# Two transformer layers with an S5 branch: a later-written input for the residual's scaling, the next layer's S5 operators and the gelu

## The chip, the cores and the metric

The kernel runs on one core of a Trainium2 chip, in one launch. The metric is the device time of that launch in microseconds (us); three runs of the kernel before are shown. Engines are called as in the profile: PE is the matrix engine (PEld its weight loads), DVE the vector engine, ACT the scalar engine, POOL is GpSimd, and SP issues most of the DMAs.

## The reference

Two layers run over 640 tokens, 128 context tokens and 512 latent ones, with 1024 channels. Each layer computes

- `h = x * (1 + scale1) + shift1`, and one product with `w_in`, whose columns are the input of the S5 branch, q, k and v of a windowed attention, q, k and v of a global attention, and three gates
- branch 0, a two-way S5 scan with small complex states, then `y = gelu(y)` and `y = y * sigmoid(y @ w_glu)`
- branch 1, the windowed attention (at most 128 tokens away, with the context's keys from a cache), and branch 2, the global attention; both have 8 heads of 64
- `merged = sum_k sigmoid(gate_k) * (branch_k @ w_br_k)` and `f = merged @ w_out`
- `x = LayerNorm(alpha * x + gate1 * f)`, then `x = LayerNorm(alpha * x + gate2 * relu(h2 @ w_up)^2 @ w_down)` with `h2 = x * (1 + scale2) + shift2`; the MLP has 4096 hidden columns

All of it is held in float32. The states and the keys and values of the context are outputs too.

## The kernel before, in words

**Tiles.** The tokens are `NT` = 5 tiles of 128: tile 0 is the context, 1 to 4 are the latent tokens. The layers are l = 0 and l = 1.

**Products.** A float32 operand is split in two rounded parts: `split` (L120) writes hi = copy(src) on ACT (L126) and lo = src - hi on DVE (L127); with `half` it also halves (L123, L124). Each product is three matmuls (hi with hi, hi with lo, lo with hi): L162 to L164 in `mm_fm`, L173 to L175 in `mm_tm`, L1247 to L1249 in the MLP's second product. `wtile` (L129) loads a raw weight tile and splits it into two `whi` and two `wlo` tiles, of which there are `WBUFS` = 4 each. A product's result goes to a p_g bank of PSUM (in the MLP to p_sc banks too).

**The order of work.** No order of the whole is written out by hand. A framework takes the program, gives each tile a buffer of its tag (`bufs` of them, handed out in the program's order), and puts every engine's instructions in one fixed order by a planned timeline, in which what comes earlier in the program has priority and what comes later fills in where nothing earlier can run. On the chip each engine's queue then runs strictly in that order, and an instruction waits for its inputs and its buffer.

**Around the gelu (`phase_a`).** In the program's order: the S5 scan, whose output is read back into `yT` (L1068); the windowed attention; the global attention (L1156), which writes `yg`; the gates of branch 1 (some were computed earlier and kept in DRAM, `AHEAD`), and branch 1's product (L1165); the gelu over `yT` in place (L1166); `split_y` into `ya` (L1168); four tiles of branch 0's gates, computed ahead and stored in DRAM (L1169); the GLU, two weight tiles and four channel tiles, each a product, a tanh on ACT into an `sg` tile of tag t640 (L1180, two such buffers) and an update of `yT` on DVE (L1182); `split_y` again (L1184); the fifth gate ahead (L1185); branch 0 (L1187), which fetches the stored gates into t640 buffers (L1111); the first gates of branch 2 into `gg`, a large tile in the buffer that `yT` had (L1188 to L1193); branch 2 (L1206), whose input is `yg`.

The attention (`attend`) works token tile by token tile, and in a tile by four pairs of heads. A pair's scores fill two p_sc banks, or three where there are five key blocks (there are three banks); row maxima on DVE (L950), their combination (L953 windowed, L958 global), the exponentials on ACT (L962, L964), transposes of P on PE (L971) into p_pt, a split of them, and the product with V. When a tile's four pairs are done, it is divided by the sums (L1001): for the global attention that is the last write of `yg[:, t]`.

**Around the MLP (`phase_b`).** After the product with `w_out` and the norm (L276 writes `x`), h2 is split into hh and hl. The MLP goes over e = 0 to 7: up(e), then down(e - 1), which from e = 1 on adds into `acc` (L1460; down(0) writes it). At e = 3 the program has the block that scales the residual, `x = x * (alpha g) + (alpha b)` in halves of 512 columns: ten multiplications (L1474) and ten additions (L1475) on DVE, with the two rows loaded by DMA and scaled by alpha on ACT (`rows`, L1220, for layer 0; `halves_of`, L1439, in four DMAs, for layer 1, where the MLP's products use a scheme with fewer multiplications). At e = 7 a like block of 20 operations, L1484 and L1485, prepares `acc` for the second norm. Layer 1's S5 operators are computed in layer 0's MLP: `both` (L1298) is a generator that `ahead()` advances one step per weight tile from down(0) on; it begins in `s5_prep` (L279) with three POOL copies (L288) and four DMAs of small inputs.

A POOL copy of one column into a tile that a DMA or another instruction then writes makes that instruction wait for what the copy reads.

Of the kernel before, what the change touches and what calls it, by code (L numbers as in the profile page):

```python
# [4 lines left out]
F32 = mybir.dt.float32  # L5
# [10 lines left out]
NT = 5  # L16
D = 1024
NCH = 84
ALPHA = (2.0 * DEPTH) ** 0.25
# [12 lines left out]
def net(tc, I, O, depth=DEPTH, dbg=None):  # L32
    nc = tc.nc
    V, S, G, T, SY = nc.vector, nc.scalar, nc.gpsimd, nc.tensor, nc.sync
    dbg = dbg or {}

    def ap(t, off, dims):
        return bass.AP(tensor=t.tensor, offset=t.offset + off, ap=[list(d) for d in dims])

    def bc(t, off, n):  # L40
        return ap(t, off, [[0, 128], [1, n]])

    def dump(name, t):
        if name in dbg:
            SY.dma_start(dbg[name], t)
# [11 lines left out]
    def pg():  # L57
        turn[0] += 1
        if mlp[0] == 2:
            return (psc, ppt, lambda: bank("g", 2), psc, ppv, ppt, lambda: bank("g", 2), psc)[turn[0] % 8]()  # L60
        return psc() if mlp[0] and turn[0] % 5 in (1, 3, 4) else bank("g", 2)
# [4 lines left out]
    def ppt():  # L66
        return bank("pt", 2)
# [61 lines left out]
    def wtile(src, K, slot=None):  # L129

        raw = raw_tile(src)
        out = []
        for i in range(2):
            if slot is not None:
                hi, lo = slot(), slot()
            else:
                hi = wp.tile([128, 512], F32R, name="whi", tag="whi", bufs=WBUFS)
                lo = wp.tile([128, 512], F32R, name="wlo", tag="wlo", bufs=WBUFS)
            cnt["w"] += 1
            split(hi, lo, raw[:, i * 512:(i + 1) * 512])  # L140
            hv, lv = (z.rearrange("p (k c) -> p k c", k=K // 2) for z in (hi, lo))
            out += [(hv[:, k], lv[:, k]) for k in range(K // 2)]
        return out

    def cols(ws, a, b):
        return [(x_[:, a:b], y_[:, a:b]) for x_, y_ in ws]
# [132 lines left out]
    def s5_prep(l, pp, pl_, keep, after=None, use=None):  # L279
# [5 lines left out]
        lre, lim, lst = t32("lre"), t32("lim"), t32("lst")  # L285
        if after is not None:
            for z in (lre, lim, lst):
                G.tensor_copy(z[:, 0:1], after)  # L288
        SY.dma_start(lre, I["lam_re"][:, l])
        SY.dma_start(lim, I["lam_im"][:, l])  # L290
        for d in range(2):
# [51 lines left out]
        k, r, a2, w = tmp  # L343
# [94 lines left out]
        for b in range(8):  # L438
# [4 lines left out]
            for r_ in range(2):  # L443
# [3 lines left out]
                p = pq()  # L447
# [66 lines left out]
    def phase_a(l, h):  # L514
# [8 lines left out]
        def f10(name):  # L523
            return qp.tile([128, 4 * 8 * NCH], F32, name=name, tag="F10", bufs=2)

        if l == 0:
# [39 lines left out]
            for g_ in range(4):  # L566
                if g_ < 3:
                    mods0(g_ + 1)
                for k in range(2 * g_, 2 * g_ + 2):
                    hf = xin.tile([128, NT, 128], F32, name="hf", tag="hf", bufs=2)  # L570
                    for t0, t1 in ((2, 5), (0, 2)):
                        p = ppt()
# [58 lines left out]
        for ft in range(4):  # L631
# [5 lines left out]
            for i, (t0, t1) in enumerate(SPLITS):  # L637
                n = (t1 - t0) * 128
                p = uacc[ft][i] if ws is None else pg()
# [178 lines left out]
        def gate(i, ft, out_fn, side=iter(())):  # L818

            ws = wtile(I["w_gate"][l, i * 8 + ft], 8)  # L820
            for t0, t1 in SPLITS:
                p = pg()
                n = (t1 - t0) * 128
                mm_fm(p[:, :n], ws, H, t0, t1)
                next(side, None)
                S.activation(out_fn(t0, t1), p[:, :n].rearrange("p (t n) -> p t n", n=128), AF.Tanh, scale=0.5)
# [212 lines left out]
        for b in range(8):  # L1039
# [8 lines left out]
            p = pg()  # L1048
# [18 lines left out]
        yT = f10("yT").rearrange("p (f t c) -> p f t c", f=4, t=8)  # L1067
# [12 lines left out]
        def t640(name):  # L1080
            return bp.tile([128, NT, 128], F32, name=name, tag="t640", bufs=2)
# [21 lines left out]
        def branch(i, acts, last=None, side=iter(()), ready={}):  # L1103
            for i2 in range(4):
                ws = wtile(I["w_br"][l, i, i2], 4)
                for f in range(2):
                    ft = 2 * i2 + f
                    pre = i == 1 or ft in ready
                    sg = mtv[:, ft] if i == 1 else ready[ft] if pre else t640("sg")
                    if i == 0 and ft < sum(AHEAD[l][4:]):  # L1110
                        SY.dma_start(sg.rearrange("p t n -> p (t n)"), s_d[l][0, ft])  # L1111
                    elif not pre:
                        gate(i, ft, lambda t0, t1: sg[:, t0:t1])
                    for t0, t1 in SPLITS:
                        p = pg()
                        n = (t1 - t0) * 128
                        mm_fm(p[:, :n], cols(ws, f * 128, f * 128 + 128), acts, t0, t1)
                        next(side, None)
                        V.scalar_tensor_tensor(sg[:, t0:t1], sg[:, t0:t1], 1.0, p[:, :n].rearrange("p (t n) -> p t n", n=128), op0=ALU.add, op1=ALU.mult)  # L1119
                    if i != 1:  # L1120
                        V.tensor_tensor(mtv[:, ft], sg, mtv[:, ft], op=ALU.add)
                    if last is not None:
                        last(ft)
# [31 lines left out]
        yg = f10("yg")[:, 0:2560].rearrange("p (t f n) -> p t f n", t=NT, f=4)  # L1155
# [7 lines left out]
        for ft in range(n1, 8):  # L1163
            gate(1, ft, lambda t0, t1: mtv[:, ft, t0:t1])
        branch(1, aw, side=mods)  # L1165
        S.activation(yT, yT, AF.Gelu_apprx_tanh)  # L1166
        dump("yT", yT)
        ya = split_y(False)  # L1168
# [2 lines left out]
        for i2 in range(2):  # L1171
            ws = wtile(I["w_glu"][l, i2], 4)
            for f in range(2):
                ft = 2 * i2 + f
                sg = t640("sg")
                for t0, t1 in SPLITS:
                    p = pg()
# [38 lines left out]
    def phase_b(l, M):  # L1216
        mp = tc.alloc_tile_pool(name=f"mp{l}", bufs=1, reuse_waits="tile")
        mlp[0] = True

        def rows(*srcs, scale=None):  # L1220

            r = mp.tile([128, 2, D], F32, name="rows", tag="rows", bufs=1)
            for i, (src, off) in enumerate(srcs):
                SY.dma_start(r[:, i], bc(src, off, D))
            if scale is not None:
                S.activation(r, r, AF.Copy, scale=scale)
            return r[:, 0], r[:, 1]
# [26 lines left out]
        x = mp.tile([128, NT, D], F32, name="x")  # L1254
        acc = mp.tile([128, NT, D], F32, name="acc")
# [26 lines left out]
        for t in range(NT):  # L1282
            p = pg()
# [14 lines left out]
        def both(l, pool, after):  # L1298
            kept = {}
            yield from s5_prep(l, pool, pool, kept, after)  # L1300
            yield from s5_tables(l, pool, kept)

        nxt = []
        if l + 1 < depth:
            nxt = [mods_steps(l + 1, range(3), lambda: mp.tile([128, 512], F32, name="mtmp", tag="mtmp", bufs=1),
                              lambda: mp.tile([128, 4, 128], F32, name="hf", tag="hf", bufs=2).rearrange("p a b -> p (a b)")), both(l + 1, mp, x[:, NT - 1, D - 1:D])]
        calls = [0]

        def ahead():
# [126 lines left out]
            def __getitem__(self, i):  # L1436
                return self.parts[i[1].start // 512]

        def halves_of(srcs, scale=None):  # L1439
            r = [Halves([mp.tile([128, 512], F32, name=n, tag=n, bufs=2) for _ in range(2)]) for n in ("gp", "rl")]  # L1440
            for z, (src, off) in zip(r, srcs):
                for i, y in enumerate(z.parts):
                    SY.dma_start(y, bc(src, off + 512 * i, 512))
                    if scale is not None:
                        S.activation(y, y, AF.Copy, scale=scale)
            return r
# [17 lines left out]
        ff = up(0)  # L1464
        for e in range(1, 8):
            if e == 3:

                if bil:
                    rg_, rb_ = halves_of(((I["ln1_g"], l * D), (I["ln1_b"], l * D)), scale=ALPHA)
                else:  # L1470
                    rg_, rb_ = rows((I["ln1_g"], l * D), (I["ln1_b"], l * D), scale=ALPHA)
                for t in range(NT):
                    for cs in (slice(0, 512), slice(512, 1024)):
                        V.tensor_tensor(x[:, t, cs], x[:, t, cs], rg_[:, cs], op=ALU.mult)  # L1474
                        V.tensor_tensor(x[:, t, cs], x[:, t, cs], rb_[:, cs], op=ALU.add)  # L1475
            if e == 7:

                if bil:
                    g2 = halves_of([(g_d[l], (2 + c) * D) for c in range(2)])
                else:  # L1480
                    g2 = rows(*((g_d[l], (2 + c) * D) for c in range(2)))
                for cs in (slice(0, 512), slice(512, 1024)):
                    for t in range(NT):
                        V.tensor_tensor(acc[:, t, cs], acc[:, t, cs], g2[0 if t == 0 else 1][:, cs], op=ALU.mult)  # L1484
                        V.tensor_tensor(acc[:, t, cs], acc[:, t, cs], x[:, t, cs], op=ALU.add)  # L1485
            nf = up(e)
            if e == 7 and bil:

                down(6, ff, (0,))
                f6 = ff  # L1490
            else:
                down(e - 1, ff)
            ff = nf
# [25 lines left out]
        if l + 1 == depth:  # L1519
            rg_, rb_ = ([mp.tile([128, 512], F32, name="lrow", tag="lrow", bufs=4) for _ in range(2)] for _ in range(2))  # L1520
# [3 lines left out]
        for t in range(NT):  # L1524
            for c in range(2):
                p = pg()
# [10 lines left out]
            else:  # L1537
                ve = ln_stat(st[t])
                o = O["xp"] if t == 0 else O["xs"][(t - 1) * 128:t * 128, :]
                for cs in (slice(0, 512), slice(512, 1024)):  # L1540
                    z = acc[:, t, cs]
# [15 lines left out]
    for l in range(depth):  # L1557
        M = phase_a(l, h)
        h = phase_b(l, M)
# [98 lines left out]
```

## Time and profile before

| | us |
|---|---|
| three runs | 2341.27, 2339.97, 2344.25 |
| median | 2341.27 |
| the profiled execution: its own time | 2345.22 |
| its span, first to last instruction | 2343.4 |
| PE busy | 2254.6 (96%) |
| DVE busy | 1568.1 (67%) |
| ACT busy | 1082.9 (46%) |
| POOL busy | 44.7 (2%) |
| mean granted clock of PE | 0.981 |

The profile is one execution. Busy time is the time in which an engine worked on at least one instruction; starts are counted from the span's beginning. The granted clock is a share of PE's full speed.

### The profile page before, as it was taken

What the parts mean: (1) busy time and instruction counts of PE and PEld (TensorE: products, weight loads), DVE (VectorE), ACT (ScalarE), POOL (GpSimd) and SP (SyncE); (2) the same over time, 40 slices, a digit from 0 to 9 for tenths busy, and PEclk for the clock granted to TensorE, in tenths of its full rate; (3) what the DMA queues carried; (4) which work ended last, traced back from release to release, by engine and by line L of the source; (5) the groups of instructions that cost most, each with busy time, mean ns of one, the idle gap of its engine ahead of it and who ended that gap; (6) DMA issues with size and microseconds to landing.
All of it is one profiled execution on the core that took longest, in us unless ns stands there. A gap on an engine that the chain in (4) does not pass through costs nothing.

```text
span 2343.4 us, 38521 instructions
## 1 busy us (share of the span) xinstructions
PE 2254.6 (96%) x14736; PEld 2040.4 (87%) x14736; DVE 1568.1 (67%) x3471; ACT 1082.9 (46%) x2572; POOL 44.7 (2%) x75
## 2 busy tenths in 40 slices
PE   7998999999998999999999999989999989999998
PEld 4997896899997988888888998989999879999986
DVE  6789954676358955455657598466763587776688
ACT  3455654674344443223224457456652356454441
POOL 0000100000000000000000001000000000000000
PEclk8998999999999999999999999999999999999999
DMA  7423366523242345344354522552212413222231
GB/s 268 119 81 106 108 179 229 198 72 98 73 154 65 94 172 175 127 156 160 135 176 142 162 63 88 158 182 77 86 53 80 171 37 99 77 77 83 83 106 62
DMA packets 124825, 283.16 MB, mean 121 GB/s; under 512 B 37057, under 2 KB 56641, under 8 KB 124641
## 3 DMA queue, kind: packets, MB, share of 16 engines
q1 hardware_dynamic: 124640, 280.70, 37.3%
q8 instruction: 116, 1.90, 0.3%
q14 instruction: 69, 0.56, 0.1%
HBM read 243.59 MB, written 41.25 MB: 122 GB/s over the span
## 4 chain that ended last, share of the span: by engine, by line
PE 82%; DVE 9%; DMA 5%; ACT 2%; issue 1%; SPq 1%; POOL 0%; DVEq 0%; ACTq 0%; POOLq 0%
PE p_g L162 8%; PE p_g L164 8%; PE p_g L163 8%; PE p_sc L1247 3%; PE p_sc L1249 3%; PE p_sc L1248 3%; PE p_sc L162 3%; PE p_sc L163 3%; PE p_sc L164 3%; PE p_pt L971 2%; PE p_g L1247 2%; PE p_g L1249 2%; PE p_g L1248 2%; PE p_g L173 2%; PE p_g L174 2%; PE p_g L175 2%
## 5 line engine op out<-in xcount | busy, mean ns | idle before, releaser
L126 ACT ACTIVATE whi<-raw 128x512 fp32r<-128x512 f32 x454 | 282.8, 631 | 408.7 <-PE p_g L1249 98.0
L127 DVE TENSOR_TENSOR wlo<-raw,whi 128x512 fp32r<-128x512 f32 x454 | 310.0, 688 | 229.7 <-ACT whi L126 220.6
L162 PE MATMUL p_g<-hh,whi 128*128 128x384 f32 (+1 forms) x1040 | 327.3, 315 | 2.3 <-ACT whi L126 1.2
L163 PE MATMUL p_g<-hl,whi 128*128 128x384 f32 (+1 forms) x1040 | 325.0, 313 | 2.8 <-DVE hl L127 2.8
L164 PE MATMUL p_g<-hh,wlo 128*128 128x384 f32 (+1 forms) x1040 | 324.4, 313 | 1.4 <-DVE wlo L127 1.2
L162 PEld LDWEIGHTS p_g<-hh,whi 128*128 128x128 f32 x1040 | 198.7, 191 | 8.0 <-ACT rl L1421 4.2
L163 PEld LDWEIGHTS p_g<-hl,whi 128*128 128x128 f32 x1040 | 198.9, 191 | 3.3 <-DVE hl L127 3.3
L164 PEld LDWEIGHTS p_g<-hh,wlo 128*128 128x128 f32 x1040 | 198.3, 191 | 2.5 <-DVE wlo L127 2.5
L162 PE MATMUL p_g<-act,whi 128*128 128x384 f32 x448 | 141.0, 315 | 5.6 <-DVE mt L1119 3.9
L127 DVE TENSOR_TENSOR pl<-p_pt,ph 128x512 fp32r<-128x512 f32 (+1 forms) x176 | 103.0, 589 | 58.1 <-ACT ph L126 44.7
L173 PE MATMUL p_g<-whi,hh 128*128 128x256 f32 x480 | 138.6, 291 | 1.1 <-DVE rt L742 0.7
L163 PE MATMUL p_g<-act,whi 128*128 128x384 f32 x448 | 139.5, 311 | 0.0
L164 PE MATMUL p_g<-act,wlo 128*128 128x384 f32 x448 | 138.7, 310 | 0.0
L174 PE MATMUL p_g<-wlo,hh 128*128 128x256 f32 x480 | 137.1, 288 | 1.1 <-DVE wlo L127 1.1
L175 PE MATMUL p_g<-whi,hl 128*128 128x256 f32 x480 | 136.7, 287 | 0.0
L163 PE MATMUL p_sc<-hl,whi 128*128 128x384 f32 (+1 forms) x384 | 121.5, 317 | 5.5 <-DVE hl L127 2.9
L126 ACT ACTIVATE ph<-p_pt 128x512 fp32r<-128x512 f32 (+1 forms) x176 | 90.7, 522 | 73.4 <-PE p_pt L971 71.3
L162 PE MATMUL p_sc<-hh,whi 128*128 128x384 f32 (+1 forms) x384 | 121.8, 319 | 0.4 <-ACT hh L126 0.4
L164 PE MATMUL p_sc<-hh,wlo 128*128 128x256 f32 (+1 forms) x384 | 120.7, 316 | 0.0
L950 DVE TENSOR_REDUCE part<-p_sc 128x1 f32<-128x384 f32 (+2 forms) x160 | 83.3, 526 | 34.2 <-PE p_sc L940 20.5
L971 PE MATMUL p_pt<-ident,P 128*128 128x128 f32 x576 | 96.6, 278 | 8.3 <-ACT P L962 6.3
L1247 PE MATMUL p_sc<-whi,ff 128*128 128x512 f32 x248 | 98.6, 400 | 0.0
(542 smaller groups left out, 5961.2 us busy)
## 6 DMA issues: line engine op xcount, KB each, us to landing
raw<-in_w_mod_dram SPq DMA_DIRECT2D x96, 512.0 KB, 3.9
raw<-in_w_up_dram SPq DMA_DIRECT2D x64, 512.0 KB, 3.7
raw<-in_w_down_dram SPq DMA_DIRECT2D x64, 512.0 KB, 3.6
raw<-in_w_gate_dram SPq DMA_DIRECT2D x48, 512.0 KB, 3.6
raw<-in_w_br_dram SPq DMA_DIRECT2D x24, 512.0 KB, 6.7
raw<-in_w_q_dram SPq DMA_DIRECT2D x16, 512.0 KB, 3.7
ctab_d<-ct SPq DMA_DIRECT2D x16, 512.0 KB, 2.6
tab<-ctab_d SPq DMA_DIRECT2D x16, 512.0 KB
```

The costliest lines, as they stand in the source:

```text
L126: S.activation(hi, src, AF.Copy)
L127: V.tensor_tensor(lo, src, hi, op=ALU.subtract)
L162: T.matmul(out, wh, tok(ah, t0, t1), start=(first and k == 0), stop=False)
L163: T.matmul(out, wh, tok(al, t0, t1), start=False, stop=False)
L164: T.matmul(out, wl, tok(ah, t0, t1), start=False, stop=(last and k == n - 1))
L173: T.matmul(out, ah, wh, start=(first and k == 0), stop=False)
L174: T.matmul(out, ah, wl, start=False, stop=False)
L175: T.matmul(out, al, wh, start=False, stop=(last and k == n - 1))
L971: T.transpose(p[:, (2 * (z - z0) + z_) * 128:(2 * (z - z0) + z_ + 1) * 128], Ps[z_][:, z * 128:(z + 1) * 128], ident)
L1247: T.matmul(banks[t], a_, wh, start=(k == 0), stop=False)
L1248: T.matmul(banks[t], a_, wl, start=False, stop=False)
L1249: T.matmul(banks[t], b_, wh, start=False, stop=(k == n - 1))
```

## The change

Four instructions or blocks are each given an input that is written later, by a small GpSimd copy into one of their operands.

- The three copies in `s5_prep` read one column of the last lo tile that up(0) writes, in place of the last column of the norm's output. The source is now a function, called when the generator starts, and `ff`, the output of up(0), is empty until then.
- A copy of one column of `yg`, token tile 4, into `yT` stands ahead of the gelu.
- The rows that scale the residual at e = 3 (layer 0) are first written by a copy that reads the last column of `acc`, token tiles 3 and 4.
- The four half rows of layer 1 are first written by copies that read the last column of `acc`, token tile 4.

```diff
@@ s5_prep
         if after is not None:
             for z in (lre, lim, lst):
-                G.tensor_copy(z[:, 0:1], after)
+                G.tensor_copy(z[:, 0:1], after())
         SY.dma_start(lre, I["lam_re"][:, l])
@@ phase_a
         branch(1, aw, side=mods)
+        G.tensor_copy(yT[:, 0, 0, 0:1], yg[:, NT - 1, 0, 0:1])
         S.activation(yT, yT, AF.Gelu_apprx_tanh)
@@ phase_b
-        def rows(*srcs, scale=None):
+        def rows(*srcs, scale=None, after=None):
             r = mp.tile([128, 2, D], F32, name="rows", tag="rows", bufs=1)
+            if after is not None:
+                G.tensor_copy(r[:, :, 0:1], after)
@@
+        ff = []
         if l + 1 < depth:
...
-both(l + 1, mp, x[:, NT - 1, D - 1:D])]
+both(l + 1, mp, lambda: ff[-1][1][:, NT - 1, 127:128].bitcast(F32))]
@@
-        def halves_of(srcs, scale=None):
+        def halves_of(srcs, scale=None, after=None):
...
+                    if after is not None:
+                        G.tensor_copy(y[:, 0:1], after)
                     SY.dma_start(y, bc(src, off + 512 * i, 512))
@@ e == 3
-                    rg_, rb_ = halves_of(..., scale=ALPHA)
+                    rg_, rb_ = halves_of(..., scale=ALPHA, after=acc[:, NT - 1, D - 1:D])
-                    rg_, rb_ = rows(..., scale=ALPHA)
+                    rg_, rb_ = rows(..., scale=ALPHA, after=acc[:, NT - 2:NT, D - 1:D])
```

## Rows read from the trace of the kernel before

**Rows 1.** The page's head and its first part.

```profile
span 2343.4 us, 38521 instructions
PE 2254.6 (96%) x14736; PEld 2040.4 (87%) x14736; DVE 1568.1 (67%) x3471; ACT 1082.9 (46%) x2572; POOL 44.7 (2%) x75
```

**Rows 2.** L1166, the gelu: duration ns min/median/max, first and last start us, forms.

```profile
L1166 ACT ACT_TABLE_LOAD  x2: 1283/1283/1283, 378.5 to 1535.4; - x2
L1166 ACT ACTIVATE yT<-yT x2: 2447/2450/2452, 379.8 to 1536.7; 128x2688 f32<-128x2688 f32 x2
```

**Rows 3.** L1001 in 340 to 700 us (layer 0) and 1490 to 1890 (layer 1).

```profile
L1001 DVE TENSOR_TENSOR yg<-yg,p_pt x5: 680/686/689, 403.1 to 574.6; 128x512 f32<-128x512 f32 x5
...
L1001 DVE TENSOR_TENSOR yg<-yg,p_pt x5: 677/687/690, 1569.8 to 1746.8; 128x512 f32<-128x512 f32 x5
```

**Rows 4.** L1180 of both layers, and L1111 of layer 0, in the same stretches.

```profile
L1180 ACT ACTIVATE sg<-p_g x8: 367/444/519, 496.6 to 518.8; 128x384 f32<-128x384 f32 x4, 128x256 f32<-128x256 f32 x4
...
L1180 ACT ACTIVATE sg<-p_g x8: 380/446/495, 1650.6 to 1671.5; 128x384 f32<-128x384 f32 x4, 128x256 f32<-128x256 f32 x4
...
L1111 SPq DMA_DIRECT2D sg<-s_d x5: 319/326/350, 512.1 to 547.1; - x5
```

**Rows 5.** L958, once per head pair, in 492 to 575 and in 1647 to 1750.

```profile
L958 DVE TENSOR_TENSOR stat<-part,ssq x7: 139/152/161, 497.8 to 556.4; 128x2 f32<-128x2 f32 x7
...
L958 DVE TENSOR_TENSOR stat<-part,ssq x8: 147/153/178, 1650.4 to 1728.6; 128x2 f32<-128x2 f32 x8
```

**Rows 6.** Windows, all instructions: us, PE, PEld, DVE, ACT, POOL busy, PEclk, DMA share, GB/s.

```profile
492.00:575.00 83.00, 82.49 (x599) 80.52 (x598) 65.60 (x135) 53.73 (x131) 0.00 (x0) 1.00 0.28 86
1647.00:1747.00 100.00, 98.56 (x712) 97.52 (x712) 70.84 (x143) 60.23 (x149) 0.00 (x0) 1.00 0.22 69
```

**Rows 7.** The same windows, instructions that touch p_g alone (no POOL column).

```profile
492.00:575.00 83.00, 61.12 (x371) 54.09 (x370) 6.54 (x14) 5.66 (x13) 1.00 0.28 86
1647.00:1747.00 100.00, 73.56 (x446) 66.77 (x447) 6.73 (x14) 6.95 (x16) 1.00 0.22 69
```

**Rows 8.** L953, once per pair of the windowed attention, in 1452 to 1480.

```profile
L953 DVE TENSOR_TENSOR stat<-part,nsink x5: 152/161/161, 1454.6 to 1477.3; 128x2 f32<-128x2 f32 x5
```

**Rows 9.** L288, the first of the three POOL copies.

```profile
L288 POOL COPY lre<-x x1: 671/671/671, 748.3 to 748.3; 128x1 f32<-128x1 f32 x1
```

**Rows 10.** Tile yT in 340 to 700: ACT's half of the split behind the gelu.

```profile
L126 ACT ACTIVATE act<-yT x8: 416/764/1146, 442.9 to 453.9; 128x128 fp32r<-128x128 f32 x4, 128x512 fp32r<-128x512 f32 x4
```

**Rows 11.** PE's waits in 1515:1560, 733:765, 1890:1920: us in total, times, longest.

```profile
PE p_pt L971 <- ACT P L962: 2.5, 1, 2.5
...
PE p_sc L163 <- DVE hl L127: 2.9, 1, 2.9
PE p_g L163 <- DVE hl L127: 1.8, 1, 1.8
...
PE p_sc L163 <- DVE mv L267: 2.6, 1, 2.6
```

**Rows 12.** Windows as in rows 6: norm to MLP, windowed attention, MLP.

```profile
745.00:765.00 20.00, 14.97 (x74) 13.65 (x73) 19.79 (x43) 8.76 (x19) 1.87 (x3) 0.83 0.11 24
1890.00:1912.00 22.00, 15.73 (x72) 13.32 (x71) 17.94 (x45) 13.60 (x28) 1.46 (x2) 0.77 0.09 25
1454.00:1478.00 24.00, 23.22 (x152) 21.45 (x153) 12.42 (x29) 13.84 (x36) 0.00 (x0) 0.86 0.42 131
800.00:830.00 30.00, 30.00 (x168) 24.47 (x167) 24.70 (x55) 12.33 (x25) 0.00 (x0) 1.00 0.44 144
2043.00:2068.00 25.00, 25.00 (x171) 24.91 (x170) 21.30 (x39) 17.57 (x36) 0.00 (x0) 1.00 0.30 89
2254.00:2279.00 25.00, 24.72 (x169) 24.46 (x168) 24.34 (x46) 14.88 (x31) 0.00 (x0) 1.00 0.38 127
```

**Rows 13.** L1474 in 730 to 770, and L1485 in 2200 to 2290.

```profile
L1474 DVE TENSOR_TENSOR x<-x,rows x10: 684/686/691, 745.2 to 759.2; 128x512 f32<-128x512 f32 x10
...
L1485 DVE TENSOR_TENSOR acc<-acc,x x10: 683/685/687, 2241.5 to 2264.8; 128x512 f32<-128x512 f32 x10
```

More of the change, by code (lines that the diff above doesn't have):

```diff
@@ L1303, in phase_b @@
         nxt = []
+        ff = []
         if l + 1 < depth:
             nxt = [mods_steps(l + 1, range(3), lambda: mp.tile([128, 512], F32, name="mtmp", tag="mtmp", bufs=1),
-                              lambda: mp.tile([128, 4, 128], F32, name="hf", tag="hf", bufs=2).rearrange("p a b -> p (a b)")), both(l + 1, mp, x[:, NT - 1, D - 1:D])]
+                              lambda: mp.tile([128, 4, 128], F32, name="hf", tag="hf", bufs=2).rearrange("p a b -> p (a b)")), both(l + 1, mp, lambda: ff[-1][1][:, NT - 1, 127:128].bitcast(F32))]
         calls = [0]
@@ L1468, in phase_b @@
                 if bil:
-                    rg_, rb_ = halves_of(((I["ln1_g"], l * D), (I["ln1_b"], l * D)), scale=ALPHA)
+                    rg_, rb_ = halves_of(((I["ln1_g"], l * D), (I["ln1_b"], l * D)), scale=ALPHA, after=acc[:, NT - 1, D - 1:D])
                 else:
-                    rg_, rb_ = rows((I["ln1_g"], l * D), (I["ln1_b"], l * D), scale=ALPHA)
+                    rg_, rb_ = rows((I["ln1_g"], l * D), (I["ln1_b"], l * D), scale=ALPHA, after=acc[:, NT - 2:NT, D - 1:D])
                 for t in range(NT):
```

## The prediction, made before the change was timed

> **What bounds the kernel now.** I read the page's sums first [rows 1]: PE is busy 2254.6 of the span's 2343.4 us, DVE 67%, ACT 46%, POOL 2%. So PE is idle for only 88.8 us in all, an edit can win no more than that, and it can lose wherever it takes from PE the matmuls that cover someone's wait. So for each edit I asked what PE does meanwhile.
>
> The instructions of the gelu's line come next [rows 2]: a table load at 378.5 and 1535.4 us, and a gelu of 2.45 us right behind it, at 379.8 and 1536.7. The scaling of the attention output, once per token tile, shows where the global attention stands [rows 3]: its last write starts at 574.6 in layer 0 and at 1746.8 in layer 1. **Today the gelu runs about 200 us before the attention ends**, in both layers. In between lies what hangs on it: the GLU's tanhs run from 496.6 and from 1650.6 [rows 4], and the first gate that was computed ahead is fetched behind them at 512.1, for branch 0. The attention's head pairs go on through all that: 7 of them from 497.8 to 556.4, and 8 from 1650.4 to 1728.6 [rows 5]. In these stretches PE is busy 82.49 of 83 us and 98.56 of 100 [rows 6], but of that 61.12 and 73.56 us are p_g products (GLU, branch and gates), not attention [rows 7]. The attention's own share is 82.49 - 61.12 = 21.4 us and 98.56 - 73.56 = 25.0 us. Covered so, a pair comes every (556.4 - 497.8) / 6 = 9.8 us; its PE work is only 21.4 / 7 = 3.1 us.
>
> **The gelu's edit, part 1: the attention loses its cover.** The copy reads token tile 4 of yg, so the gelu waits for the attention's last write. Queued behind the gelu, by data or by buffers, are split_y, the GLU (its two weight tiles fill all four weight slots, so the later gate's weights can't come first), the stored gates of branch 0 (their t640 buffers are handed out after the GLU's), branch 0 (wants ya), and the gates of branch 2 (their buffer is yT's). What doesn't hang on it, branch 1 and the four gates ahead, is used up when the GLU starts today, at 496 and 1650. So from there on the attention runs alone. A pair takes all three p_sc banks, so the next pair's scores can't start before its exps are through: alone it is bound by a chain of engines. The nearest row is the window attention, with at most 512 keys: five pairs from 1454.6 to 1477.3 [rows 8], 22.7 / 4 = 5.7 us each. The bounds of a lone pair are 3.1 us (PE never idle) and 9.8 us (no faster than today); I take 5.7, being the nearest row, and for my own range 5.7 x 640 / 512 = 7.1 for the five key blocks, and 4.5, as far below. Alone, layer 0 then takes 5.8 us to its first pair, 6 x 5.7, and an estimated 10 us to the last write (18.9 today, from 556.4 to 575.3, half of it as for the pairs): 50.0 us, in which PE does 21.4. Lost: 28.6. Layer 1: 3.4 + 7 x 5.7 + 10 - 25.0 = 28.3. **Together +56.9 us** (13 p - 17.2: 41 at p = 4.5, 75 at 7.1; 23 and 110 at the outer bounds).
>
> **Part 2: the gelu's own chain stands bare.** Behind the last write come the copy, a table load, the gelu and the split of its output, and PE has nothing. POOL copy 0.67 (as the three of today, [rows 9]), table load 1.28, gelu 2.45 [rows 2], and the split, whose 8 ACT halves average 0.764 us [rows 10]: 6.1, of which PE can start on the first quarter, so I take 4.0: 8.4 us a layer, **+16.8** (11 to 22). Today attention and gates hide all of it. The later gate still covers the step from GLU to branch 0.
> The table load's row shows 1.283 us, and the gelu follows at once. The Trainium skill's page "ScalarE: Activation LUTs", section "What ACT_TABLE_LOAD costs", adds a drain of about 1.38 us to every switch; by it this part would be 2.8 us more. No drain shows here, so I leave it out.
>
> **What the gelu's move gives back.** At the attention's start PE waits once for the exp behind the gelu, 2.5 us in layer 1 [rows 11]; with the lower clock behind such waits I take -5 for both layers (-2 to -7).
>
> **Residual scaling, at its old place.** The step from norm to MLP is short of DVE. PE waits 2.9 and 1.8 us there in layer 0 and 2.6 in layer 1 for splits that DVE owes [rows 11]. DVE is busy 19.79 of 20 us in 745 to 765, at a granted clock of 0.83, and 17.94 of 22 in layer 1, at 0.77 [rows 12], because the 20 operations of 0.69 us stand in its queue (the first ten: 745.2 to 759.2, [rows 13]). Behind acc they come some 140 us later. I take -5 a layer, **-10** (-3 to -15): PE's idle 5.0 and 6.3 us in these stretches is the cap without the clock.
>
> **At its new place** 20 operations of some 0.62 us net, 12.3 us, land at e = 3 on DVE, with its two row loads behind the copies (6 POOL copies in all, 4.0 us on an engine 2% busy; behind them on POOL stand only other copies). In layer 1 DVE has 21.30 of 25 us there, PE prefetched full. The nearest row is the same kind of block for the second norm: its ten adds lie at 2241.5 to 2264.8 [rows 13], DVE busy 24.34 of 25, PE still 24.72. So little: I take **+2** for both (0 to +10).
>
> **Next layer's S5 operators.** The three copies move from the norm's output to the last split of up(0); SP's queue holds the row loads behind them, and POOL and the S5's own DVE operations move along. PE is 30.00 of 30 in 800 to 830 with DVE at 24.70 [rows 12]; this is filler and stays filler. 0 (-2 to +2).
>
> **The sum.** 56.9 + 16.8 - 5 - 10 + 2 = +60.7 us on the profiled execution's 2345.22: 2405.9. The median of the runs, 2341.27, stands 3.95 lower, so **2402 us**. Its own range: all terms low 41 + 11 - 7 - 15 + 0 - 2 = +28, all high 75 + 22 - 2 - 3 + 10 + 2 = +104; not all at once, 2371 to 2436.
>
> **Rivals.**
> *Faster: the attention quickens where filler recedes.* If the schedule drops filler behind the attention as soon as the gelu is late, tiles 1 to 4 could be through before the other filler is used up: they take 16 pairs from 403.1 [rows 3], so the point is (496 - 403.1) / 16 = 5.8 us a pair. Then filler covers the gelu's chain too, and -5 - 10 + 2 = -13 stays: 2328 us. For it: 5.8 is no less than the lone pace of 5.7. Against: with filler it ran at (574.6 - 403.1) / 16 = 10.7, and the same filler stands there up to 496. 0.12.
> *About the same: the change doesn't cost the cover.* If buffers are handed out in the order of use, the later gates could come ahead of the GLU; 28.6 us of the p_g work [rows 7] would do. Then 16.8 - 5 - 10 + 2 = +4: 2345. Against: today no such gate runs ahead of the GLU. 0.06.
> *Slower still: the clock falls while the attention is alone.* In the window attention it was 0.86 on average, PE busy 23.22 of 24 [rows 12]. If half of each pair's 3.1 us ran at the lower level (1.2 GHz in place of 2.4), a pair would take 1.5 us more, 13 of them 20: 2422 (with all of it, 2442). 0.12.
> The skill's page "TensorE: Matmul & The Clock Gate", section "HAM oscillation", describes this: short bursts of matmuls between waits fall back to half speed again and again. The row at 0.86 agrees in kind.
>
> **How the numbers follow.** Forecast 0.70, the rivals 0.12, 0.06 and 0.12. The prediction is 2402 us. The range reaches from the case with the cover kept, 2345, to 2436; out of it lie the fast rival and the forecast's and the clock's far ends, together under 2 in 10. About 0.2%, 4.7 us, is what a measurement of this kernel can tell from no change. Faster: 0.13, the fast rival and the chance that the losses come out small and the gains large. Same: 0.05, most of the case at 2345. Slower: 0.82.
>
> **What would show it.** Right: the gelu starts within some 2 us of the last L1001 write; before it PE idles some 28 us a layer, with waits on the exps; pairs come every 5 to 7 us in the last third of the attention; PE idles 8 us more between that write and the GLU; PE's waits for the hl splits after the norm are gone, and the residual's operations lie beside up(3) with no idle PE. Wrong: a pair period near 10 to the end with PE busy (cover found elsewhere), an attention that ends before the four gates do, or a PE wait at e = 3.

## The result, and the profile after

The changed kernel takes 2403.35 us (median of 6 runs, 2396.37 to 2405.82) against 2342.35 (6 runs). The medians lie 61.0 us apart; all runs taken together put the ratio at 1.0247, 95% interval 1.0235 to 1.0258, which is 57.9 us. The profiled execution's span is 2402.5 us, 59.1 more than before [rows 1].

The page's head and first part, of the changed kernel:

```profile
span 2402.5 us, 38564 instructions
PE 2281.7 (95%) x14736; PEld 2053.2 (85%) x14736; DVE 1575.7 (66%) x3471; ACT 1082.3 (45%) x2571; POOL 45.6 (2%) x82
```

PE does the same 14736 matmuls. It is idle for 2402.5 - 2281.7 = 120.8 us, 32.0 more than before, and busy for 27.1 us more: the loss is in part idle time and in part the same matmuls counted as busy for longer. No run separates the two parts of that second share: matmuls run at a lower granted clock, and one with nothing behind it counts with its whole duration (0.28 us for 256 columns, where in the full queue before the lone stretch the next one starts 0.12 us later). The windows show both idle time and clock. These are the stretches from the last other product to the attention's last write, each with the stretch behind it (all instructions, columns as in [rows 6]):

```profile
496.00:546.00 50.00, 35.49 (x201) 30.46 (x200) 30.47 (x69) 31.97 (x85) 0.06 (x1) 0.86 0.04 14
546.00:557.00 11.00, 6.74 (x24) 6.32 (x24) 5.42 (x8) 7.82 (x10) 0.12 (x1) 0.53 0.01 1
1678.00:1733.00 55.00, 37.66 (x222) 31.60 (x219) 34.16 (x77) 36.01 (x95) 0.00 (x0) 0.91 0.00 1
1733.00:1743.00 10.00, 5.40 (x23) 4.91 (x24) 5.51 (x9) 7.80 (x9) 0.18 (x1) 0.66 0.00 0
```

The two lone stretches for instructions that touch p_g, as in [rows 7]:

```profile
496.00:546.00 50.00, 0.00 (x0) 0.00 (x0) 0.00 (x0) 0.40 (x1) 0.86 0.04 14
1678.00:1733.00 55.00, 0.00 (x0) 0.00 (x0) 0.00 (x0) 0.00 (x0) 0.91 0.00 1
```

Where p_g products took three quarters of PE's time [rows 7] there is now none: for 50 and 55 us PE has only the attention, at a granted clock of 0.86 and 0.91, and DMA nearly stands still (shares of 0.04 and 0.00). Behind them, after a gap in PE's work (below), the clock is 0.53 and 0.66, near the lower of its two levels (1.2 of 2.4 GHz).

The gelu's copy, by its line:

```profile
L1166 POOL COPY yT<-yg x2: 184/184/185, 545.9 to 1733.3; 128x1 f32<-128x1 f32 x2
```

The attention's pairs in the two lone stretches, as in [rows 5]:

```profile
L958 DVE TENSOR_TENSOR stat<-part,ssq x6: 149/160/161, 499.6 to 532.7; 128x2 f32<-128x2 f32 x6
...
L958 DVE TENSOR_TENSOR stat<-part,ssq x7: 151/160/161, 1679.8 to 1718.1; 128x2 f32<-128x2 f32 x7
```

ACT around the attention's end in layer 0 (timeline: start, us, instruction, in brackets the idle time before it and what ended it); the gelu's line is L1167 now [rows 2]:

```profile
543.82 0.38 ACT L985 ACTIVATE yt<-p_pv 64x256 f32<-64x256 f32 x1
544.21 1.28 ACT L1167 ACT_TABLE_LOAD   x1
546.15 2.44 ACT L1167 ACTIVATE yT<-yT 128x2688 f32<-128x2688 f32 x1 [0.66 <-POOL yT L1166]
548.63 2.69 ACT L126 ACTIVATE act<-yT 128x128 fp32r<-128x128 f32 x4
```

PE's timeline, its first matmul after the attention, in layer 0 and in layer 1, and the writes of L1001 in layer 1 (those of layer 0 are shown with e9 below):

```profile
550.06 0.90 PE L162 MATMUL p_g<-act,whi 128*128 128x384 f32 x2 [6.67 <-ACT act L126]
...
1737.40 0.90 PE L162 MATMUL p_g<-act,whi 128*128 128x384 f32 x2 [6.75 <-ACT act L126]
...
L1001 DVE TENSOR_TENSOR yg<-yg,p_pt x5: 678/686/689, 1602.7 to 1732.4; 128x512 f32<-128x512 f32 x5
```

A lone pair takes (532.7 - 499.6) / 5 = 6.6 us and (1718.1 - 1679.8) / 6 = 6.4. Then PE stands idle for 6.67 us (6.75 in layer 1) until the first GLU product. Of that, 2.4 us still belong to the attention's end: its last write lasts until 545.8 and 1733.1, and from there to the product it is 4.25 and 4.34 us.

The attention's start, up to where the other filler ends, as windows of all instructions; the kernel before, then the changed one, whose layer 1 runs 28 us later:

```profile
340.00:496.00 156.00, 148.27 (x1043) 125.64 (x1042) 90.62 (x190) 86.24 (x201) 0.00 (x0) 0.99 0.57 189
1480.00:1650.00 170.00, 161.52 (x1158) 157.73 (x1157) 98.17 (x203) 95.56 (x222) 0.00 (x0) 0.98 0.44 137
...
340.00:496.00 156.00, 150.13 (x1057) 126.42 (x1055) 88.46 (x186) 78.07 (x199) 0.00 (x0) 0.99 0.58 189
1508.00:1678.00 170.00, 163.81 (x1195) 160.25 (x1194) 97.75 (x205) 89.23 (x223) 0.00 (x0) 0.99 0.45 140
```

Here, where the gelu stood before, PE is idle for 1.9 and 2.3 us less.

In the MLPs PE's waits (a wait of layer 1 for ACT's part of acc, 2.5 us, which stood there before too, is left out) show what the residual's edits did, layer 0's step from norm to MLP (770 to 805), layer 1's (1950 to 1980) and layer 1's e = 3 (2095 to 2135):

```profile
PE p_pt L242 <- ACT hf L248: 3.6, 2, 2.9
...
PE p_sc L163 <- DVE hl L127: 0.3, 1, 0.3
PE p_g L163 <- DVE hl L127: 0.2, 1, 0.2
...
PE p_pt L1372 <- DVE wlo L127: 1.7, 1, 1.7
PE p_sc L1372 <- DVE wlo L127: 1.6, 1, 1.6
PE p_g L1370 <- ACT whi L126: 0.6, 1, 0.6
PE p_pt L1370 <- ACT whi L126: 0.6, 1, 0.6
```

The residual's multiplications, by their line (L1480 now), as in [rows 13]:

```profile
L1480 DVE TENSOR_TENSOR x<-x,rows x10: 685/688/693, 944.6 to 950.0; 128x512 f32<-128x512 f32 x10
L1480 DVE TENSOR_TENSOR x<-x,gp x10: 683/684/691, 2101.3 to 2106.8; 128x512 f32<-128x512 f32 x10
```

The waits of [rows 11] are gone in layer 0 (the 3.6 us for hf stood there before as well), and in layer 1 0.5 us are left. But layer 1 has four new ones, 4.5 us together, where its 20 operations now stand; at layer 0's new place PE has none.

### The profile page after: what moved, and what is told of

It is laid out like the page before. It is cut to its first block, busy times and chain, and to the rows that moved or that the text cites. A ratio compares the mean times of both kernels' runs of the same rounds, so it can differ in the third digit from the quotient of the medians.

```text
span 2402.5 us, 38564 instructions
## 1 busy us (share of the span) xinstructions
PE 2281.7 (95%) x14736; PEld 2053.2 (85%) x14736; DVE 1575.7 (66%) x3471; ACT 1082.3 (45%) x2571; POOL 45.6 (2%) x82
## 4 chain that ended last, share of the span: by engine, by line
PE 78%; DVE 8%; issue 7%; DMA 4%; ACT 2%; SPq 1%; POOL 0%; DVEq 0%; ACTq 0%; POOLq 0%
PE p_g L162 9%; PE p_g L164 9%; PE p_g L163 9%; PE p_sc L1250 3%; PE p_sc L1252 3%; PE p_sc L1251 3%; PE p_pt L971 2%; PE p_sc L162 2%; PE p_sc L163 2%; PE p_sc L164 2%; PE p_g L173 2%; PE p_g L174 2%; PE p_g L175 2%; PE p_g L1250 2%; PE p_g L1251 2%
## 5 line engine op out<-in xcount | busy, mean ns | idle before, releaser
L162 PE MATMUL p_g<-act,whi 128*128 128x384 f32 x448 | 144.2, 323 | 23.4 <-ACT act L126 13.4
L163 PE MATMUL p_g<-act,whi 128*128 128x384 f32 x448 | 141.7, 316 | 0.4 <-DVE act L127 0.4
L126 ACT ACTIVATE ph<-p_pt 128x512 fp32r<-128x512 f32 (+1 forms) x176 | 90.2, 521 | 85.3 <-PE p_pt L971 84.7
L971 PE MATMUL p_pt<-ident,P 128*128 128x128 f32 x576 | 102.6, 291 | 14.8 <-DVE pl L127 6.4
L162 PEld LDWEIGHTS p_g<-act,whi 128*128 128x128 f32 x448 | 87.3, 195 | 29.8 <-ACT act L126 13.8
```

What stands on the lines that cost most here:

```text
L126: S.activation(hi, src, AF.Copy)
L162: T.matmul(out, wh, tok(ah, t0, t1), start=(first and k == 0), stop=False)
L163: T.matmul(out, wh, tok(al, t0, t1), start=False, stop=False)
L971: T.transpose(p[:, (2 * (z - z0) + z_) * 128:(2 * (z - z0) + z_ + 1) * 128], Ps[z_][:, z * 128:(z + 1) * 128], ident)
```

## The experiments

Theory: the gelu's edit costs the attention its cover (part 1) and lays its own chain bare (part 2); the others win a little. Rivals: a late gelu costs whatever covers it; the bare chain is most of it; the other edits cost time too. A ratio is against the runs of the kernel before beside it, with its 95% interval; the us behind a ratio are worked out from it.

**The gelu's copy alone, and all but it.**

```diff
 e1: before, with
+        G.tensor_copy(yT[:, 0, 0, 0:1], yg[:, NT - 1, 0, 0:1])
         S.activation(yT, yT, AF.Gelu_apprx_tanh)
 e2: the changed kernel without that line
```

> Only the gelu's copy (token tile 4) is kept. Theory: the whole loss lies in the two attention stages, which in the changed kernel are 36.2 and 30.7 us longer than before (net of the gain at the attention's start), so 2342 + 67 = about 2409 us, 6 to 9 us above the changed kernel. Rival: the three other edits cost time too (the residual behind acc stalls layer 1's up(3)), then this one lies below the changed kernel, at 2395 or less.

> The other three edits without the gelu's copy. Theory: only what the MLP stages won in the changed kernel stays, 7.9 us in layer 0 and 0.7 in layer 1: 2342.4 - 8.6 = about 2334 us. Rival: those 8 us came from the later gelu's shift of the order, then 2342 or more.

e1: 2407.56 us, ratio 1.0285 (1.027 to 1.0299), or +66.7 us. e2: 2332.63 us, 0.9971 (0.996 to 0.9982), or -6.8. Together 59.9, between the 57.9 and 61.0 of the change itself. All the loss is the gelu's.

**An earlier gate.**

```diff
 e3, e4: before, with
+        G.tensor_copy(yT[:, 0, 0, 0:1], yg[:, 1, 0, 0:1])     (e4: yg[:, 3, ...])
```

> The kernel before with a copy ahead of the gelu that reads token tile 1 of yg, not tile 4 (written at 456 and 1624 us in the kernel before, where other filler lasts to 496 and 1650). Theory: what costs is the lost cover, not a late gelu as such; filler lasts beyond the gelu's chain, so no loss, and the attention's start wins up to 5 us a layer: 2333 to 2342, taken 2337 us. Rival: any gelu amid the attention costs (two table loads and 2.45 us on ACT between exps): 2350 or more.

> The kernel before with a copy ahead of the gelu that reads token tile 3 of yg. Theory: the attention is alone from where the other filler ends (about 496 and 1678 us in the changed kernel) to tile 3's write (521 and 1705 there), half the stretch of the changed kernel, and the gelu's chain is covered by tile 4's pairs: about half of the lost 29 us in each layer, less 5: 2342 + 24 = 2366 us (2355 to 2378). Rival (the bare chain behind the attention carries most of the loss): 2350 or less. Rival (any gate past tile 1 costs all of it): 2400 or more.

e3: 2341.75 us, 1.0002 (0.9992 to 1.0011): a gelu in the middle of the attention costs nothing while filler lasts, so lateness as such is not the cause. It wins nothing that shows either: a wait behind the gelu moved along with it. PE now waits for an exp, up to 467 us, in the window 440 to 480:

```profile
PE p_sc L939 <- ACT P L962: 2.1, 1, 2.1
```

e4: 2391.72 us, 1.0232 (1.0213 to 1.0251), far above the 2366 that I expected. ACT shows why, from the gelu's table load to the end of the split (lines left out are exps, accumulators and splits of the pairs):

```profile
519.53 1.28 ACT L1167 ACT_TABLE_LOAD   x1
520.82 2.44 ACT L1167 ACTIVATE yT<-yT 128x2688 f32<-128x2688 f32 x1
523.17 0.85 ACT L126 ACTIVATE ph<-p_pt 128x512 fp32r<-128x512 f32 x2
524.04 1.28 ACT L962 ACT_TABLE_LOAD   x1
...
527.74 1.42 ACT L126 ACTIVATE act<-yT 128x128 fp32r<-128x128 f32 x2
529.04 0.60 ACT L126 ACTIVATE ph<-p_pt 128x512 fp32r<-128x512 f32 x1
529.52 1.46 ACT L126 ACTIVATE act<-yT 128x128 fp32r<-128x128 f32 x2
530.85 0.62 ACT L126 ACTIVATE ph<-p_pt 128x512 fp32r<-128x512 f32 x1
531.33 2.77 ACT L126 ACTIVATE act<-yT 128x128 fp32r<-128x128 f32 x4
...
539.23 0.77 ACT L1181 ACTIVATE sg<-p_g 128x384 f32<-128x384 f32 x2
```

The gelu's chain shares ACT with the lone pairs and each delays the other: the copy's data are there at 518, the first GLU tanh comes at 539.2. With the copy alone on tile 4 (e1) it came at 549.9. A gate some 21 us earlier (that write stood at 538.9 in e1) shortened the lone stretch by only 11, and the time by 16 us for both layers. I had counted the chain as covered by the pairs at no cost; but both need ACT.

**More filler.** The changed kernel with more of branch 0's gates computed ahead of the GLU:

```diff
-AHEAD = ((0, 1, 4, 2, 4, 1), (1, 0, 1, 2, 4, 1))
+AHEAD = ((0, 1, 4, 2, 7, 1), (1, 0, 1, 2, 7, 1))
```

> The changed kernel, but all eight of branch 0's gates are computed ahead (seven before the GLU, one after; four and one in the changed kernel): some 21 us of independent PE work a layer is moved ahead of the GLU, no work is added but three more stores and fetches. Theory (lost cover): with this filler a pair goes at 9.8 us and PE is full; 21 us cover some 3 of the 7 lone pairs, each of which loses about 3.6 us alone: 2403 - 22 = about 2381 us (2370 to 2390). If each filler us saved one of PE's lost us: 2361. Rival (a late gelu costs whatever covers it): 2400 or more.

2380.67 us, 1.0163 (1.0148 to 1.0179): 22.7 us under the changed kernel (21.1 if each is taken against the runs of the kernel before beside it), with the same gelu gate. Its windows in layer 0, all instructions, before and after the filler's end:

```profile
496.00:531.00 35.00, 33.57 (x249) 33.20 (x249) 20.43 (x45) 20.29 (x53) 0.00 (x0) 1.00 0.24 78
531.00:556.00 25.00, 17.19 (x92) 13.61 (x90) 13.05 (x30) 16.34 (x42) 0.18 (x1) 0.86 0.06 22
```

With cover PE is busy 33.57 of 35 us at full clock; where it ends PE falls to 17.19 of 25 at 0.86. That shows the cover to be the cause, by dose.

**The chain alone.** The gelu early, and the copy in front of the split behind it:

```diff
-        G.tensor_copy(yT[:, 0, 0, 0:1], yg[:, NT - 1, 0, 0:1])
+                if ft == 0 and not half:
+                    G.tensor_copy(a[:, 0, 0:1], yg[:, NT - 1, 0, 0:1])      (in split_y)
```

> The gelu runs early as in the kernel before (its copy is gone), and the copy that reads yg's token tile 4 goes into the first tile of the split behind it: the lone stretch stays, the bare chain loses the gelu (2.44 us) and keeps copy and split. Theory (lone attention and bare chain are separate terms): PE's gap behind the attention falls from 6.7 us to about 4 in each layer, 2403 - 6 = about 2397 us (2393 to 2401). Rival (the gelu's place itself carries the loss): 2375 or less. Rival (the chain isn't on the path): 2402 or more.

2399.11 us, 1.0247 (1.0233 to 1.0261): the median is 4.2 under the changed kernel's, but the ratio is the same, so the forecast 6 us are not shown. What is clear is the trace: PE's gap behind the attention is 3.85 us in both layers (6.67 and 6.75 with the gelu in it), and the time stays near 2400.

```profile
545.93 0.90 PE L162 MATMUL p_g<-act,whi 128*128 128x384 f32 x2 [3.85 <-ACT act L126]
```

So the gelu's place isn't the loss; the lone stretch is.

**What sets the lone pair's pace.** The changed kernel with a third bank freed for scores, or for transposes:

```diff
 e9:
-                    p5 = psc() if nb > 4 else None
+                    p5 = pg() if nb > 4 else None
 e12:
-                        p = ppt()
+                        p = pg() if z0 == 4 else ppt()
```

> The changed kernel, but the scores against key blocks 4 and 5 (p5) take a p_g bank, idle in the lone stretch, in place of the third p_sc bank: a pair holds two of three p_sc banks, so the next pair's first scores needn't wait for its last exp. Theory as predicted (a lone pair is bound by the three p_sc banks): its period falls from 6.6 us towards 5, 13 pairs win some 20 us: about 2383 us. Rival (the trace of the changed kernel: PE waits there for pl, DVE's half of the split of the transposed P, so the chain transposes, ph, pl, PV sets the pace): 2398 to 2408, periods as before.

> The changed kernel, but the third group of a pair's transposes (key block 5) goes to a p_g bank, so a pair needs no p_pt bank twice. As with the scores in p_g banks, the filler's products are pushed behind the attention, so the whole is slower than the changed kernel (2420 to 2460 us); what counts is the time from one token tile's last write to the next, 23.9 to 31.3 us alone in the changed kernel and 26.7 to 31.6 in layer 0 with the scores moved. Theory A (two p_pt banks, freed only by DVE's pl, set the lone pace): 20 to 23 us a tile. Theory B (the latency of the chain exp, transposes, ph, pl, PV through three engines sets it, whatever the banks): 24 us or more.

e9: 2453.98 us, 1.0486 (1.0466 to 1.0506). e12: 2483.43 us, 1.0607 (1.0567 to 1.0648). Both are slower: the filler's products need the p_g banks, and buffers are handed out in the program's order, so they stand behind the attention (in e9 36 of PE's 263 matmuls from 410 to 470 us touch p_g, and they are the moved scores). That I had not foreseen for e9, and its time missed both forecasts. They still measure a lone tile. The writes of L1001 in the changed kernel (489 to 560), in e9 (410 to 470) and in e12 (400 to 600):

```profile
L1001 DVE TENSOR_TENSOR yg<-yg,p_pt x3: 678/687/689, 490.0 to 545.1; 128x512 f32<-128x512 f32 x3
```

```profile
L1001 DVE TENSOR_TENSOR yg<-yg,p_pt x3: 675/686/689, 414.0 to 468.5; 128x512 f32<-128x512 f32 x3
```

```profile
L1001 DVE TENSOR_TENSOR yg<-yg,p_pt x4: 686/688/689, 420.5 to 505.8; 128x512 f32<-128x512 f32 x4
```

A tile of four pairs takes 55.1 / 2 = 27.6 us, 54.5 / 2 = 27.3 and 85.3 / 3 = 28.4. Single tiles lie between 23.9 and 32.8 us in the three runs, and none came down to the 20 to 23 us that a freed bank should have given. Neither bank alone sets the pace. PE's waits in the lone stretch of the changed kernel (496 to 546) agree:

```profile
PE p_pv L979 <- DVE pl L127: 5.4, 7, 1.4
PE p_pt L971 <- DVE pl L127: 3.3, 2, 1.7
PE p_pv L978 <- DVE yg L987: 2.4, 3, 1.4
PE p_pv L978 <- ACT ph L126: 0.2, 1, 0.2
PE p_sc L948 <- ACT P L962: 0.2, 1, 0.2
```

For a p_sc bank PE waits 0.2 us of 50; most of its waits are for DVE's half of the split transposes. That the latency of exp, transposes, split and product sets the pace is what is left, but no run shortened that chain, so it is argued and not shown. The single p_pv bank (2.4 us for L987), the two pl buffers and the lower clock weren't taken apart either.

**The residual's two edits and the S5's.** Each residual edit alone; then e2 with layer 1's copies reading what down(1) writes in its first half; then that without the S5 edit.

```diff
 e5: only rows(..., after=...)      e6: only halves_of(..., after=...)
 e7: e2, with
-    halves_of(..., after=acc[:, NT - 1, D - 1:D])
+    halves_of(..., after=acc[:, NT - 1, 0:1])
 e11: e7, with
-    both(l + 1, mp, lambda: ff[-1][1][:, NT - 1, 127:128].bitcast(F32))
+    both(l + 1, mp, lambda: x[:, NT - 1, D - 1:D])
```

> Only the edit on layer 0's residual rows is kept. Theory: it is what wins in layer 0's step from norm to MLP (4.7 us of PE waits gone, and the lower clock behind them): 7 us, 2340.8 - 7 = about 2334 us, most of the 8.2 us that the three edits won without the gelu's. Rival: the S5 operators' edit or layer 1's has its part, then 2337 or more.

> Only the edit on layer 1's half rows is kept. Theory: the 5 us that it wins between norm and MLP it gives back at e = 3, where PE waits 4.4 us for DVE's and ACT's splits behind the 20 residual operations: 2340 us, no difference that can be told (within 4 us). Rival: the two don't balance, then 2335 or less, or 2345 or more.

> The three edits without the gelu's, and layer 1's copies read the first column of acc's token tile 4, which down(1) writes in its first half, not the last column, which it writes at its end. Theory: what layer 1's edit gives back is that its 20 operations land at the start of up(3), where products wait for DVE's splits; half of down(1) earlier DVE is about half idle, so the 4.3 us of waits go: 2332.6 - 5 = about 2327.5 us, and no PE wait beside those operations. Rival: the waits only move along: 2332 or more.

> As the kernel with the residual's two edits, layer 1's on the first half of acc, but the S5 operators' edit undone. Theory: the S5 edit is worth next to nothing (PE idles 0.3 us less after the norm): 2329.9 + 0.5 = about 2330.5 us (2328 to 2333). Rival: it carries what the two residual edits don't add up to in the three, 2 us or more: 2332 or more.

e5: 2335.16 us, 0.9973 (0.9961 to 0.9984), or -6.3. e6: 2342.33 us, 1.0005 (0.9995 to 1.0015): given back, as expected. e7: 2329.94 us, 0.9953 (0.994 to 0.9965). e11: 2329.98 us, 0.9951 (0.9937 to 0.9965), so the S5 edit is worth nothing that shows. PE's waits at layer 1's e = 3, in e2 (2020 to 2050), and in e7 (2015 to 2050):

```profile
PE p_sc L1371 <- DVE wlo L127: 1.6, 1, 1.6
PE p_pt L1371 <- DVE wlo L127: 1.5, 1, 1.5
PE p_pt L1369 <- ACT whi L126: 0.6, 1, 0.6
PE p_g L1369 <- ACT whi L126: 0.6, 1, 0.6
```

```profile
PE p_g L1369 <- DVE acc L1465: 1.4, 1, 1.4
PE p_pt L1369 <- ACT whi L126: 0.3, 1, 0.3
```

4.3 us of waits became 1.7, not none, and the time fell 2.7 us under e2, not 5, with intervals that still touch. **e7 and e11 beat both kernels**, at some 11 us less than before (0.9953 and 0.9951).

## Why the prediction was right

It gave 2402 us; 2403.35 was measured. The mechanism is the one forecast, but that the time came out to within 2 us is in part luck: two terms of the gelu's edit missed by some 8 us each, in opposite directions. By its steps:

- **Part 1, the lost cover**: the cause is right, the size too small. The lone stretches were forecast at 50.0 and 53.3 us, counted from 492 and 1647; 50 and 55 came, from 496 and 1678. Inside, a pair took 6.5 us, not 5.7 (the clock of 0.86 to 0.91 the third rival spoke of has its part in that), and the last pair to the write took 13.1 and 15.0 us, not 10; but 6 and 7 pairs were left, not 7 and 8. So the stretches held less of the attention's own work: 201 and 222 matmuls, where the forecast took off 21.4 and 25.0 us for 599 - 371 = 228 and 712 - 446 = 266 [rows 6, rows 7]. At the same 0.094 us each that is 18.9 and 20.9 us, and an estimated 31.1 + 34.1 = 65.2 us were lost, not 56.9. The sign "PE idles some 28 us a layer" failed: it idled 14.5 and 17.3 us, because its own matmuls were busy for 35.5 and 37.7 us, not 21.4 and 25.0. Nor did it wait on the exps, and the reason given for the pace, that a pair takes all three p_sc banks, is not what the runs show: PE waits for DVE's pl.
- **Part 2, the bare chain**: 8.4 us a layer forecast from the last write to the first product, 4.25 and 4.34 measured, 8.6 for 16.8 together. The copy took 0.18 us, not 0.67, and the table load, 1.28, ran at 544.21, ahead of the gelu's wait; so it is no part of the chain.
- **What the gelu's move gives back**: -5 forecast; PE's idle time in the attention's starts fell by 1.9 + 2.3 = 4.2 us. e3 can't show it, for there the gelu still stands among the exps and the wait moves along with it. The gelu's edit as a whole was forecast at 56.9 + 16.8 - 5 = 68.7 us; e1 measured 66.7.
- **Residual**: -5 in layer 0 was right (-6.3 with the new place). In layer 1 the waits went as forecast, but the new place was mis-sized: +2 for both layers, where up(3) of layer 1 alone waited 4.5 us, at a granted clock of 0.96 from 2095 to 2135. A PE wait at e = 3 was one of the prediction's own signs of being wrong. The nearest row that I took, the e = 7 block [rows 13], stands beside products that didn't wait; here up(3) had just begun and DVE's splits stood behind the block. The range, up to +10, held it. (There are five POOL copies for the rows, not six: one in layer 0 and four in layer 1.)
- **S5 operators**: 0, and 0.
- **The rivals**: the attention didn't quicken enough under filler (tile 4's write was at 545, not 496); no gate came ahead of the GLU; the lower clock came, and it is in the 8 us that part 1 lost beyond the forecast, but part 2 took them back. Of the row at 0.86 that the third rival leans on, a finer look shows one fall only: the windowed attention ran at 0.50 from 1454 to 1460 us, after PE had been idle for most of 1452 to 1454, and at 1.00 from 1462 on. The falling back again and again is what the changed kernel's lone stretch shows: 0.50 from 499 to 502, 1.00 from 505 to 511, 0.50 from 523 to 529, 1.00 from 532 to 544.

## What to carry to other kernels

A wait that ties filler to the end of the stage it fills costs the cover, and the price is the stage's lone pace, not the waiting instruction: find when the other filler is used up, and gate no later than that. A block that is moved to where its engine looks free must be set against the start of the products beside it, not their mean; half a step earlier the new waits fell from 4.3 to 1.7 us here. Before giving a stage another bank, look what else draws on that bank, for buffers handed out in program order push it back.

## What the runs showed of the hardware that I had not expected

The same POOL copy of one column takes two durations: 0.67 us beside DVE's residual block in the kernel before [rows 9], 0.18 where DVE had just ended (the gelu's copy above, and the copies of L288 themselves in the changed kernel, at 813 us). The Trainium skill's page "GPSIMD Engine Reference", section "Specifications", says that GpSimd's SBUF interfaces are shared with DVE, with contention where a DVE instruction has two SBUF inputs; the residual's multiplications have two, so the rows agree, though no run here tested it.

A table load doesn't wait for what its activation waits for: it ran 1.94 us ahead of the gelu, while ACT had nothing else.
